# Gates by seven products of half-depth operands, with piecewise sums on VectorE and weight splits on GpSimd

## The chip, the cores and the metric

The kernel runs on one core of one Trainium2 chip. The metric is the device time of one launch in microseconds, the median of three runs: 2691.48 us for the kernel before (2688.23 to 2693.27). In the views, PE is TensorE (matmuls), PEld its weight loads, DVE is VectorE, ACT ScalarE, POOL GpSimd and SP SyncE, which issues most DMAs.

## What is computed

A decoder block on 2048 tokens of width 1024, in float32, cut here to what the change touches:

```
h = rmsnorm(x)
proj = h @ w_in                       # q, k, v, u, z, gate_a, gate_b
gate_a, gate_b = sigmoid(proj[GA0:GB0]), sigmoid(proj[GB0:IN_WIDTH])   # 1024 columns each
y_attn = dilated_attention(q, k, v)   # 3 groups of 4 heads, merged by a softmax over groups
y_gmlp = gelu(u) * spatial(layernorm(gelu(z)))
merged = gate_a * (y_attn @ w_branch_attn) + gate_b * (y_gmlp @ w_branch_gmlp)
x = x + rmsnorm(merged @ w_out)
x = x + rmsnorm(relu(rmsnorm(x) @ w_mlp_in)**2 @ w_mlp_out)
```

The change concerns the gates before their sigmoid: 2048 tokens by 1024 channels by 2048 columns.

## The kernel before

**Numbers in two parts.** TensorE takes operands that are rounded when written as `fp32r`. To keep float32's accuracy an operand is split in a high part (a rounded copy) and a low part (the rest): `split` (L66) writes the one on ACT or POOL (L70, L72) and the other on DVE or POOL (L78). A product of two operands is then three matmuls, high by high, high by low and low by high (L95 to L97). A group of three such matmuls, 128x128 weights on 512 columns, is called a step below. `h`, normalised and transposed, is kept split in SBUF as `hT`, one tile of 4 MB for each chunk `c` of 512 tokens; two such tiles fit. The tokens of chunks 0 and 1 are also kept in DRAM, unsplit (`hTd`), and come back by `reload_h` (L232), which splits them on POOL.

**The stages.** First (0 to some 500 us) the chunks are normalised and q, k and v are computed for each half of the tokens. Then comes the stage of gates and attention (some 500 to 1000 us), the merge of the attention groups (`combine`), the u and z of the first half, the gated merge, and the last two matrix products of the MLP, whose products are already formed by seven products.

**Filler.** Attention alone would leave TensorE waiting for exponentials. So the products of u, z and the gates are written as a generator, `filler` (L528), of which `steps(n)` takes the next n steps. The 16 gate blocks of 128 columns each, in two halves of the tokens, are 512 steps: for each block and chunk eight steps over the depth of 1024, summed in one PSUM bank, copied out by ACT (`gt`, L549) and stored in DRAM (`gated`, L551). Weights `w_g` come in blocks of 512 KB; POOL writes the high and DVE the low part.

**The attention units.** There are 48 units (three groups g, four chunks c, four heads j). A turn of the loop makes scores `s` of unit n, then one step, then the transposes `pT` of unit n-1, six steps (L781), its product with v (`pv`), two steps, and its last transposes `po`, which DVE sums (L709). Between, DVE adds the mask and takes the maxima (L653, L657), turns them into the bias `nm` (L660), ACT takes the exponentials (L663), copies `pT` (`ph`, L688, and `pf`, L696) and DVE makes its low part (L689). q and k of unit n+2 are loaded at each turn.

**Combine.** Behind the last unit `combine` (L714) loads the outputs `A` of all three groups for a chunk (L717, 528 KB each), works out the weights of the groups (`M`, `E`, `Z`, L720 to L733), sums them (L737 to L740) and TensorE transposes the mean (`yt`, L745). Steps (33, 21, 20, 24) stand ahead of the four chunks' transposes (L801).

**What sets the order.** TensorE runs in the order in which the program is written. The instructions of the other engines, SP's DMAs among them, are ordered by a scheduler from its own estimate of times, unless a stretch is bound by `behind()`, which keeps its instructions behind those already issued. Each engine then runs its list strictly in that order, SP too: a store that waits holds the loads behind it.

## Time and profile before

| | |
|---|---|
| median of 3 runs | 2691.48 us (2688.23 to 2693.27) |
| profiled execution | 2690.6 us |
| its span (first to last instruction) | 2688.7 us |
| granted TensorE clock over the span | 0.998 of full speed |
| DMA | 431.77 MB, 161 GB/s over the span |
| gates' copies on ACT (L549) | 64, 37.8 us |
| gates' low parts on DVE (L78) | 30, 45.1 us |
| gates' high parts on POOL (L72) | 32, 34.1 us |

The span is one execution taken by the profiler. Matmuls are pipelined: the duration given for one (390 ns for 128x512) overlaps its neighbours, so the time that one costs is the distance between two starts. A busy engine is not by itself a bound; what counts is whether TensorE, busy 99% of the span, has to wait. "DMA share" is the mean busy share of the core's 16 DMA engines.

### The profile page before, as it was taken

To read this page: it belongs to the slowest core of one execution; us is meant where nothing else is said; L and a number is where in the kernel's file an instruction comes from. 1 tells how busy PE (TensorE), PEld (TensorE's weight loads), DVE (VectorE), ACT (ScalarE), POOL (GpSimd) and SP (SyncE) were. 2 spreads that over 40 slices of the span, in tenths; PEclk is the share of its full clock that TensorE was granted. 3 is DMA by queue.
4 is the path that set the end of the run, shared out by engine and by line. 5 is a ranking of instruction groups with operands and counts; after the bars stand their busy time and mean duration, and the time that the engine had idled before them with its cause. 6 is when DMAs were issued, how large, how long until landed. Compare 5 with 4: busy or idle time off the path is not lost. (4 is left out here: it accounts for less than half of the span.)

```text
span 2688.7 us, 34842 instructions
## 1 busy us (share of the span) xinstructions
PE 2660.5 (99%) x12674; PEld 2225.8 (83%) x12674; DVE 1586.6 (59%) x2677; ACT 1052.1 (39%) x2149; POOL 975.7 (36%) x837
## 2 busy tenths in 40 slices
...
GB/s 272 167 143 183 153 141 211 103 189 201 173 252 203 219 152 195 185 181 147 180 250 250 141 205 163 186 171 129 110 145 118 87 55 87 93 84 86 90 110 211
DMA packets 299197, 431.77 MB, mean 161 GB/s; under 512 B 52817, under 2 KB 166225, under 8 KB 299026
## 3 DMA queue, kind: packets, MB, share of 16 engines
q1 hardware_dynamic: 226864, 370.48, 43.4%
q10 hardware_dynamic: 64178, 32.06, 4.0%
...
## 5 line engine op out<-in xcount | busy, mean ns | idle before, releaser
L1637 PE MATMUL ya<-T_spots,s 128*128 128x512 f32 x1176 | 289.3, 390 | 1.0 <-ACT T_spots L70 0.5
L1637 PEld LDWEIGHTS ya<-T_spots,s 128*128 128x128 f32 x1176 | 220.7, 188 | 47.4 <-ACT T_spots L70 0.9
L70 ACT ACTIVATE s<-sraw 128x768 fp32r<-128x768 f32 (+1 forms) x184 | 127.2, 696 | 330.3 <-POOL sraw L1438 155.8
L78 DVE TENSOR_TENSOR s<-sraw,s 128x512 fp32r<-128x512 f32 x172 | 184.2, 1095 | 8.5 <-ACT s L70 7.2
L1112 PE MATMUL aa<-B,A 128*128 128x512 f32 x768 | 182.1, 390 | 0.9 <-ACT xs L1126 0.9
L1112 PEld LDWEIGHTS aa<-B,A 128*128 128x128 f32 x768 | 144.0, 188 | 31.0 <-ACT xs L1126 1.3
L1637 PE MATMUL yc<-T_spots,s 128*128 128x512 f32 x624 | 159.7, 389 | 0.0
L72 POOL TENSOR_SCALAR w_g<-w_g_r 128x1024 fp32r<-128x1024 f32 x32 | 34.1, 1082 | 344.7 <-PE g L97 286.7
L1083 POOL TENSOR_TENSOR s<-w1r 128x512 f32<-128x512 f32 x32 | 42.9, 1342 | 311.9 <-DVE S L78 261.6
L95 PE MATMUL x<-hT_a,wq 128*128 128x512 f32 x384 | 149.8, 390 | 0.0
L96 PE MATMUL x<-hT_a,wq 128*128 128x512 f32 x384 | 149.6, 390 | 0.0
L97 PE MATMUL x<-hT_a,wq 128*128 128x512 f32 x384 | 149.6, 390 | 0.0
L709 DVE TENSOR_REDUCE o<-po 128x256 f32<-128x512 f32 x48 | 33.1, 691 | 184.9 <-PE po L708 184.9
L1637 PEld LDWEIGHTS yc<-T_spots,s 128*128 128x128 f32 x624 | 117.2, 188 | 24.3
L70 ACT ACTIVATE hl<-r 128x512 fp32r<-128x512 f32 x48 | 30.4, 632 | 238.1 <-POOL r L307 89.1
L78 POOL TENSOR_TENSOR T_spots<-w2r,T_spots 128x512 fp32r<-128x512 f32 x70 | 104.5, 1520 | 7.3 <-ACT T_spots L70 7.3
L95 PE MATMUL g<-hT_b,w_g 128*128 128x512 f32 x256 | 104.7, 409 | 0.0
L95 PE MATMUL o<-wo,mg 128*128 128x512 f32 x256 | 101.3, 396 | 3.4 <-DVE g L899 2.4
L95 PE MATMUL g<-hT_a,w_g 128*128 128x512 f32 x256 | 104.3, 407 | 0.0
L78 DVE TENSOR_TENSOR A<-w1r,A 128x512 fp32r<-128x512 f32 x61 | 62.6, 1026 | 68.6 <-ACT A L70 68.6
L70 ACT ACTIVATE S<-w1r 128x512 fp32r<-128x512 f32 x96 | 60.1, 629 | 106.3 <-PE ac L1112 63.9
L97 PE MATMUL o<-wo,mg 128*128 128x512 f32 x256 | 100.6, 393 | 0.0
(390 smaller groups left out, 7195.5 us busy)
## 6 DMA issues: line engine op xcount, KB each, us to landing
w1r<-in_w_mlp_in_dram SPq DMA_DIRECT2D x64, 512.0 KB, 3.7
sraw<-sd SPq DMA_DIRECT2D x128, 256.0 KB, 3.3
...
qq<-qk SPq DMA_DIRECT2D x96, 256.0 KB, 4.9
w_g_r<-in_w_in_dram SPq DMA_DIRECT2D x32, 512.0 KB, 4.8
gated<-gt SPq DMA_DIRECT2D x64, 256.0 KB, 3.3
...
sd<-u ACTq DMA_DIRECT2D x63, 256.0 KB, 3.8
```

The source lines that it names most:

```text
L70: act.activation(hi, src, AF.Copy)
L72: pool.tensor_scalar(hi, src, 1.0, 1.0, op0=OP.mult, op1=OP.mult)
L78: (pool if lo_eng == "pool" else dve).tensor_sub(lo, src, f32(hi))
L95: pe.matmul(ps, lh, rh, start=start, stop=False)
L96: pe.matmul(ps, lh, rl, start=False, stop=False)
L97: pe.matmul(ps, ll, rh, start=False, stop=stop)
L709: dve.tensor_reduce(ot[:, :, j * 64:(j + 1) * 64], po.rearrange("p (b h e) -> p b e h", b=4, h=2), axis=AX.X, op=OP.add)
L1083: pool.tensor_add(s1, a21, a22)
L1112: pe.matmul(p, w[:, l, k, :], h[:, r, k, :], start=i in (1, 6, 5) and not k and not n, stop=k == 3 and n == 2, skip_group_check=True)
L1637: pe.matmul(p, s[:, l], w[r], start=i in (1, 2, 5) and not m and not o, stop=m == 1 and o == 2, skip_group_check=True)
```

## The change

The gates are computed half by half of the tokens as a product of matrices of two by two blocks, with seven block products in place of eight. The blocks halve the depth (channels 0 to 511 and 512 to 1023), the columns (the two 128-column parts `m` of each of eight 256-column weight blocks `n`) and the tokens (two chunks). Each product has four steps, so there are 2 x 7 x 8 products and 448 steps.

- **Phases.** The products are taken in phases (1, 2), (6, 7), (5, 3), (4), each for all eight `n`, so that one phase needs one or two token operands. While one phase runs, `operand` loads those of the next into the other of two 4 MB places (`opA`, `opB`): split token blocks for products 1 to 3 from `hbd` (2 MB each), and sums of token blocks for the others from `tgd` (1 MB each). The latter are split on arrival by ACT (L70, 128x1024) and POOL (L78), two of each for an operand.
- **Pieces.** Each product's weights are a piece of 128x512 (256 KB, rows of 512 bytes), loaded four products ahead and split three products ahead, both parts on POOL.
- **Evacuation.** Products 1 and 2 are copied by ACT (32 copies); the five others are added by DVE to what an earlier product left (80 additions of 128x512). 1 and 2, 6 and 7, 5 and 3 lie in pairs, and products 1, 6, 5 and 4 start a PSUM bank, in which 2, 7 and 3 go on.
- **Sums ahead.** In the first part `pre_step` makes the sums of weight blocks (`sgd`, `s1gd`) and of token blocks (`tgd`): 32 turns, each with a load, four operations of 128x(256 or 2x128) on DVE and stores on POOL's queue. They are handed out one at each v block of the second half, two at each q or k product, and two at the end.
- **Tokens kept.** `keep_cols` now keeps all four chunks unsplit (16 more copies on ACT and stores), `prenorm_cols` also stores split tokens (`hbd`), and `reload_h` loads them split: 4 MB for a chunk in place of 2, and nothing to split.
- **Steps.** A turn of the attention loop takes 8 steps from the fourth unit on (5 in place of 6 between `pT` and `pv`), and `combine` takes (28, 18, 17, 19). u of the first half runs chunk by chunk.

The core of the diff:

```diff
...
-    hT_d = dtile([2, P, KT, 512], "hTd")
+    hT_d = dtile([4, P, KT, 512], "hTd")
+    hb_d = dtile([4, P, 2, KT, 512], "hbd")
+    tg_d = dtile([2, P, 4, 4, 512], "tgd")
+    sg_d = dtile([8, P, 2, 4, 256], "sgd")
+    s1g_d = dtile([8, P, 4, P], "s1gd")
...
+        if i == 3:
+            ks = slice(4 if c == 3 else 0, KT)
+            if c != 2:
+                for o in range(2):
+                    sp.dma_start(hb_d[c][:, o, ks], f32(h)[:, o, ks])
...
-            split_in(hT[c][:, :, k:k + 2], hT_d[c, :, k:k + 2, :], None, "pool", "pool")
+            for o in range(2):
+                sp.dma_start(f32(hT[c])[:, o, k:k + 2], hb_d[c][:, o, k:k + 2])
...
+        def pre_t(half, k, j):
+            w = pre.tile([P, 5, 256], F32, name=f"pt{half}{k}{j}", tag="pre")
+            tsl = slice(j * 256, (j + 1) * 256)
+            for c in range(2):
+                sp.dma_start(w[:, 2 * c:2 * c + 2], hT_d[2 * half + c][:, k::4, tsl])
+            yield
+            b11, b21, b12, b22 = (w[:, n] for n in range(4))
+            dve.tensor_sub(b11, b12, b11)
+            dve.tensor_sub(b12, b22, b12)
+            dve.tensor_sub(b22, b22, b11)
+            dve.tensor_sub(b21, b21, b22)
+            yield
+            pool.dma_start(tg_d[half][:, :, k, tsl], w[:, :4])
+            yield
+        def pre_s(n, k):
+            w = pre.tile([P, 5, 256], F32, name=f"ps{n}{k}", tag="pre")
+            both = w[:, :4].rearrange("p (h k) c -> p h (k c)", h=2)
+            sp.dma_start(both, a["w_in"][13 + n].rearrange("p (h k) c -> p h k c", h=2)[:, :, k:k + 2].rearrange("p h k c -> p h (k c)"))
+            yield
+            a11, a21, a12, a22 = (w[:, 2 * kk:2 * kk + 2, m * P:(m + 1) * P] for kk in range(2) for m in range(2))
+            s1 = w[:, 4].rearrange("p (k c) -> p k c", k=2)
+            dve.tensor_add(s1, a21, a22)
+            dve.tensor_sub(a21, a11, a21)
+            dve.tensor_sub(a11, s1, a11)
+            dve.tensor_sub(a12, a12, a11)
+            yield
+            pool.dma_start(sg_d[n][:, :, k:k + 2].rearrange("p h k c -> p h (k c)"), both)
+            pool.dma_start(s1g_d[n][:, k:k + 2], s1)
+            yield
+        halves = [[(h_, k, j) for k in range(4) for j in range(2)] for h_ in range(2)]
+        makers = [lambda n=n, k=k: pre_s(n, k) for n in range(8) for k in (0, 2)]
+        makers[12:12] = [lambda z=z: pre_t(*z) for z in halves[0] + halves[1]]
+        flow = []
+        def pre_step():
+            with behind():
+                if makers:
+                    flow.append(makers.pop(0)())
+                for g in reversed(flow):
+                    next(g)
+                if len(flow) == 3 or not makers:
+                    flow.pop(0)
...
+                if half:
+                    pre_step()
...
                 qk_pair(rp, w, g, which, 2 * half, ropes[2 * half])
+                pre_step()
...
                 qk_pair(rp, w, g, which, 2 * half + 1, ropes[2 * half + 1], between)
+                pre_step()
+        pre_step()
+        pre_step()
...
-    queue += [(13 + n, "g", n, 1) for n in range(8)] + [(13 + n, "g", n, 0) for n in range(8)]
+    queue += [(13, "g", 0, 1)]
     queue += [(9, "u", 0, 0), (10, "u", 1, 0), (11, "z", 0, 0), (12, "z", 1, 0)]
...
+    PHASES = ((1, 2), (6, 7), (5, 3), (4,))
...
+    PIECES, SPLITS, LAST = 4, 3, 104
+    seq = [(half, i, n) for half in (1, 0) for ops in PHASES for i, n in lagged(ops)]
+    g_ = dict(raw={}, w={}, b={})
+    def piece(t):
+        if t >= len(seq):
+            return
+        half, i, n = seq[t]
+        raws = g_["raws"]
+        r = raws[t % 4] if t < 8 else raws[4 + (t - LAST) % 5] if t >= LAST else raws[(t - 4) % 6]
+        if i < 3:
+            src = w_src(13 + n, i - 1)[:, :, :P]
+        elif i == 5:
+            src = s1g_d[n]
+        else:
+            kk, m = {6: (0, 0), 7: (0, 1), 3: (1, 0), 4: (1, 1)}[i]
+            src = sg_d[n][:, kk, :, m * P:(m + 1) * P]
+        sp.dma_start(r.rearrange("p (k c) -> p k c", k=4), src)
+        g_["raw"][t] = r
+    def split_piece(t):
+        if t >= len(seq):
+            return
+        if t == 4:
+            g_["spots"].append(wp.tile([P, 4, 2, 4, P], F32R, name="spots1", tag="w", bufs=3))
+        at_ = t % 4 if t >= LAST else t % 8
+        w = g_["spots"][at_ // 4][:, at_ % 4]
+        split(w[:, 0], w[:, 1], g_["raw"].pop(t).rearrange("p (k c) -> p k c", k=4), "pool", "pool")
+        g_["w"][t] = w
+    def operand(half, i, slot):
+        c = 2 * half
+        g_["b"][half, i] = slot
+        if i in (1, 2, 3):
+            src = hb_d[c + (i == 3)][:, :, (0, 4, 4)[i - 1]:][:, :, :4]
+            for o in range(2):
+                sp.dma_start(f32(slot)[:, o], src[:, o])
+            return []
+        src = tg_d[half][:, (5, 4, 7, 6).index(i)]
+        for k in range(0, 4, 2):
+            sp.dma_start(f32(slot)[:, 1, k:k + 2], src[:, k:k + 2])
+        return [(slot, k) for k in (0, 2)]
+    def gates_ahead():
...
+        for t in range(PIECES):
+            piece(t)
+        for t in range(SPLITS):
+            split_piece(t)
+    def gates():
+        bank, todo = {}, []
+        slots = [None, hp.tile([P, 2, 2, 4, 512], F32R, name="opB", tag="hT", bufs=2)]
...
+        g_["b"].update({(1, 1): hT[2][:, :, :4], (1, 2): hT[2][:, :, 4:]})
+        phases = [(half, ops) for half in (1, 0) for ops in PHASES]
+        starts, t = {}, 0
+        for n, (half, ops) in enumerate(phases):
+            starts[t] = n
+            t += 8 * len(ops)
+        for t, (half, i, n) in enumerate(seq):
+            if t in starts:
+                ph, t0 = starts[t], t
+                if ph + 1 < len(phases):
+                    s = (ph + 1) % 2
+                    if not slots[s]:
+                        slots[s] = hp.tile([P, 2, 2, 4, 512], F32R, name="opA", tag="hT", bufs=2)
+                    for j, i2 in enumerate(phases[ph + 1][1]):
+                        todo += operand(phases[ph + 1][0], i2, slots[s][:, j])
+                else:
+                    reload_h(0)
+                    want(5)
+            elif todo and (t - t0) % 3 == 1 and t > t0 + 1:
+                w, k = todo.pop(0)
+                with behind():
+                    split(w[:, 0, k:k + 2], w[:, 1, k:k + 2], f32(w)[:, 1, k:k + 2], "act", "pool")
+            piece(t + PIECES)
+            split_piece(t + SPLITS)
+            if i in (1, 6, 5, 4):
+                bank[n] = psum_mm(f"g{half}{i}{n}")
+            p, w, h = bank[n], g_["w"].pop(t), g_["b"][half, i]
+            for k in range(4):
+                for m, (l, r) in enumerate(((0, 0), (0, 1), (1, 0))):
+                    pe.matmul(p, w[:, l, k], h[:, r, k], start=i in (1, 6, 5, 4) and not k and not m,
+                              stop=k == 3 and m == 2, skip_group_check=True)
+                if t == 2 and late:
+                    sz_out(*late.pop(0))
+                yield
...
+            x, z = xs[n], zs[:, n]
+            if i == 1:
+                act.activation(x, p, AF.Copy)
+            elif i == 2:
+                act.activation(z, p, AF.Copy)
+                o = z, 0, 0
+            elif i == 6:
+                dve.tensor_add(z, x, p)
+            elif i == 7:
+                dve.tensor_add(x, x, p)
+            elif i == 5:
+                v = vs[n % 3]
+                dve.tensor_add(v, x, p)
+                o = v, 1, 1
+            elif i == 3:
+                dve.tensor_add(z, z, p)
+                o = z, 0, 1
+            else:
+                dve.tensor_add(x, x, p)
+                o = x, 1, 0
+            if i in (2, 5, 3, 4):
+                c = 2 * half + o[2]
+                sp.dma_start(gate_d[n * 2 + o[1], :, c * 512:(c + 1) * 512], o[0])
     def filler():
...
+            if kind == "g":
+                yield from gates()
+                continue
...
+                if not half and (ci, n) == (0, 0):
+                    reload_h(1)
...
-            steps(6 if n > 1 else 9)
+            steps((6 if n < 4 else 5) if n > 1 else 9)
...
-        steps((33, 21, 20, 24)[n])
+        steps((28, 18, 17, 19)[n])
...
```

At three places the lists of the engines show what moved. The first is an attention unit on ACT early in the stage, in the phase of products 1 and 2, from the copy of one `pv` to the next. Names: `ph` and `pf` are the copies of `pT`, `e` the exponentials, `gt` (before) and `ga`, `gz` (now) the gates' evacuation. Before:

```order
L704 ACTIVATE pvs_4450<-pv_4442 128x512
L688 ACTIVATE ph_4498<-pT_4493 128x512
L663 ACTIVATE e_4464,o_3746<-e_4464,nm_4479 128x128
L663 ACTIVATE e_4464,o_3746<-e_4464,nm_4479 128x256 x3
L688 ACTIVATE ph_4505<-pT_4501 128x256
L549 ACTIVATE gt_4516<-g_4432 128x512
L696 ACTIVATE pf_4508<-pT_4501 128x128
L704 ACTIVATE pvs_4549<-pv_4541 128x512
```

Now:

```order
L904 ACTIVATE pvs_4731<-pv_4723 128x512
L700 ACTIVATE gz<-g_4618 128x512
L70 ACTIVATE opB<-opB 128x1024
L888 ACTIVATE ph_4787<-pT_4782 128x512
L863 ACTIVATE e_4745,o_4055<-e_4745,nm_4760 128x128
L863 ACTIVATE e_4745,o_4055<-e_4745,nm_4760 128x256 x3
L888 ACTIVATE ph_4794<-pT_4790 128x256
```

The gates' copy of the one unit stands ahead of `ph` now, not ahead of `pf`, and an operand's split stands with it.

The second is SP's list behind the last unit's output (`att_76`), where combine's loads of `A` stand. Before:

```order
L583 DMA att_76<-o_8002 128x1056 [waits DMAHW6_49,DVE_49]
L551 DMA gated<-gt_8701 128x512 [waits DMAHW7_49,Activation_49]
L717 DMA A_8614<-att_74 128x4x264 [waits DMAHW6_49,DMAHW0_49,PE_49]
L717 DMA A_8614<-att_75 128x4x264 [waits DMAHW1_49]
L717 DMA A_8614<-att_76 128x4x264 [waits DMAHW2_49]
```

Now:

```order
L718 DMA gated<-gx_4365 128x512 [waits DMAHW1_49,DVE_49]
L783 DMA att_76<-o_8402 128x1056 [waits DMAHW2_49,DVE_49,Activation_49]
L718 DMA gated<-ga_4489 128x512 [waits DMAHW3_49,DVE_49]
L718 DMA gated<-ga_4490 128x512 [waits DMAHW4_49,DVE_49]
L91 DMA w_u_r_9190<-in_w_in_dram 128x1024 [waits DMAHW5_49,Pool_49]
L917 DMA A_9047<-att_74 128x4x264 [waits DMAHW6_49,DMAHW2_49]
L917 DMA A_9047<-att_75 128x4x264 [waits DMAHW7_49]
L917 DMA A_9047<-att_76 128x4x264 [waits DMAHW0_49]
```

One gate store stood between the output and the loads; now there are two and a load of `w_u`, and ahead of them the reload of a chunk's tokens.

The third is DVE's list there, from the last sum of `po` (L709, now L909) to combine's first operation on `A` (`M`, L720, now L920). Before:

```order
L709 TENSOR_REDUCE o_8002<-po_8551 128x4x64
L709 TENSOR_REDUCE o_8002<-po_8602 128x4x64
L78 TENSOR_TENSOR w_u_8877<-w_u_r_8878,w_u_8877 128x1024
L78 TENSOR_TENSOR w_u_8877<-w_u_r_8882,w_u_8877 128x1024
L720 TENSOR_TENSOR M_8618<-A_8614 128x16
```

Now:

```order
L909 TENSOR_REDUCE o_8402<-po_9035 128x4x64
L714 TENSOR_TENSOR ga_4489<-ga_4489,g_9028 128x512
L714 TENSOR_TENSOR ga_4490<-ga_4490,g_9129 128x512
L714 TENSOR_TENSOR ga_4491<-ga_4491,g_9144 128x512
L714 TENSOR_TENSOR ga_4492<-ga_4492,g_9159 128x512
L78 TENSOR_TENSOR w_u_9189<-w_u_r_9190,w_u_9189 128x1024
L714 TENSOR_TENSOR ga_4493<-ga_4493,g_9174 128x512
L920 TENSOR_TENSOR M_9051<-A_9047 128x16
```

Five sums of gate products and a weight split stand ahead of `M`, where two weight splits did.

53 lines of the change are left out of this document (34 added, 19 removed).

## Prediction

> **What bounds the kernel now.** I read the page first, then who waits for whom on TensorE, then stretches of the span.
>
> ```profile
> PE 2660.5 (99%) x12674; PEld 2225.8 (83%) x12674; DVE 1586.6 (59%) x2677; ACT 1052.1 (39%) x2149; POOL 975.7 (36%) x837
> DVE 0%; issue 0%; ACT 0%; DVEq 0%
> ```
>
> TensorE is busy 99% of the span. The chain that ended last names only work at 0%, so it says nothing; what counts is the number of matmuls and the places where TensorE has nothing to do. In the gate and attention stage (560 to 1000 us) the view of waits has almost none:
>
> ```profile
> PE pT L683 <- DVE o L709: 1.3, 2, 0.6
> PE pv L702 <- DVE ph L689: 0.3, 1, 0.3
> ```
>
> That is 1.6 us in 440, and no better cover in this stage can win more than that. A matmul left out there is a gain of its own pitch, as long as the other engines and the DMAs still keep up. The pitch comes from a full stretch that has 128x512 matmuls alone; columns are busy us and counts for PE, PEld, DVE, ACT, POOL, then granted clock, DMA share, GB/s:
>
> ```profile
> 1650.00:1700.00 50.00, 50.00 (x222) 41.45 (x221) 22.28 (x30) 25.97 (x44) 11.00 (x8) 1.00 0.45 137
> 560.00:700.00 140.00, 139.04 (x818) 121.06 (x817) 58.56 (x178) 64.31 (x195) 8.28 (x8) 1.00 0.61 188
> 700.00:850.00 150.00, 149.37 (x864) 129.53 (x863) 68.37 (x202) 67.98 (x211) 42.33 (x28) 1.00 0.74 220
> 850.00:985.00 135.00, 134.89 (x749) 115.10 (x749) 47.69 (x189) 53.56 (x170) 8.25 (x8) 1.00 0.64 177
> 750.00:800.00 50.00, 50.00 (x291) 43.48 (x290) 21.43 (x67) 23.89 (x76) 34.07 (x20) 1.00 0.84 272
> ```
>
> 50 us / 222 = 0.225 us a matmul (the 390 ns that the page gives for one is its pipelined length).
>
> **What is removed.** Gates took 16 x 2 x 2 x 8 x 3 = 1536 matmuls; seven products of half the depth take 2 x 7 x 8 x 4 x 3 = 1344. 192 x 0.2252 us = **43.2 us** less, all in a stage where TensorE never rests. That is the gain if all else is covered. The profiled execution took 2690.6 us (its span 2688.7, 1.9 around it), 0.9 under the median, so the floor is 2690.6 - 43.2 = 2647.4 us.
>
> **Evacuation and splits.**
>
> ```profile
> L549 ACT ACTIVATE gt<-g 128x512 f32<-128x512 f32 x64 | 37.8, 592 | 62.8 <-PE g L97 42.6 <-issue 10.0 <-DMA ygd<-sb 4.8
> L78 DVE TENSOR_TENSOR w_g<-w_g_r,w_g 128x1024 fp32r<-128x1024 f32 x30 | 45.1, 1522 | 46.3 <-POOL w_g L72 46.3
> L1642 DVE TENSOR_TENSOR acc_yt<-acc_yt,ya 128x512 f32<-128x512 f32 x72 | 48.4, 684 | 24.2 <-PE ya L1637 24.2
> L72 POOL TENSOR_SCALAR yt<-yt x6: 614/618/880, 1083.6 to 1092.3; 128x512 fp32r<-128x512 f32 x6
> L78 POOL TENSOR_TENSOR yt<-yt x6: 1272/1292/1341, 1084.6 to 1094.1; 128x512 fp32r<-128x512 f32 x6
> ```
>
> DVE loses 45.1 us of splits and gains 80 additions from PSUM, 80 x 0.684 = 54.7 us: even. ACT loses 64 and gains 32 copies, about -19 us, and gains 16 operand splits of 128x1024 (an estimate from the 0.592 us of half that width: 1.05 us). POOL gains most: 112 pieces x (0.618 + 1.292) = 214 us and 16 operand splits of 2.4. Spread over the stage (some 385 us) POOL is busy about 65%; the stretch 750:800 has it at 34 us of 50 and TensorE at 50.00, so its mere load costs nothing.
>
> What POOL can do is hold DVE. In the three rows of `nm` below, the same 128x4 operation takes 0.17 us with POOL idle, and 0.86 and 1.94 us with POOL at work; it ends when POOL's instruction does:
>
> ```profile
> 703.70 0.17 DVE L660 TENSOR_SCALAR nm<-o 128x4 f32<-128x4 f32 x1
> 769.00 0.86 DVE L660 TENSOR_SCALAR nm<-o 128x4 f32<-128x4 f32 x1
> 778.28 1.94 DVE L660 TENSOR_SCALAR nm<-o 128x4 f32<-128x4 f32 x1
> 777.81 4.75 POOL L78 TENSOR_TENSOR w_g<-w_g_r,w_g 128x1024 fp32r<-128x1024 f32 x2
> 708.05 0.88 PE L702 MATMUL pv<-ph,v 128*128 128x256 f32 x6
> 707.38 0.27 ACT L696 ACTIVATE pf<-pT 128x128 f32<-128x128 f32 x1
> ```
>
> Behind `nm` on ACT stand the exponentials and `pf`, and `pv` waits for `pf`. In this unit `pf` is ready at 707.65, and its first use is the end of the `pv` row's six matmuls, at 708.76: 1.1 us to spare, of which the gate copy ahead of `pf` on ACT takes 0.5. The change takes a step of three matmuls (0.68 us) from between `pT` and `pv`, and in most phases the copy too. So about 0.9 us is left against a hold of at most 1.3 us (a piece) or 2.4 us (an operand split). The bounds: nothing, since the delayed units of 769 to 788 us show no wait; or 0.4 us in each of 32 units and 1.5 us at each of 16 operand splits, 37 us. Only a part of the units meets a POOL instruction at its start, and the last 16 units use `pf` another way, with more room. I take **4 us**, nearer the lower row.
>
> The Trainium skill (GPSIMD Engine Reference, Key points) says that GpSimd shares its SBUF interfaces with VectorE and contends with DVE instructions in a 2-port mode or with two SBUF inputs. The rows of `nm` agree for the first kind. By the rule as it stands the piecewise sums, with two SBUF inputs each, would be slowed as well; at one and a half times their length this adds some 22 us to DVE in a part where it idles far more, and changes the sum by nothing.
>
> **DMA.** In the three stretches above the DMAs are busy 85 + 111 + 86 = 283 us of 425 and move 83 MB.
>
> ```profile
> q1 hardware_dynamic: 226864, 370.48, 43.4%
> q10 hardware_dynamic: 64178, 32.06, 4.0%
> ```
>
> Packets of 500 bytes (q10) take 0.040 x 2688.7 x 16 / 64178 = 27 ns, 3.3 us per MB on 16 engines; q1 as a whole 3.15 us per MB. The gates' pieces are 112 x 0.262 = 29.4 MB in packets of 512 bytes, 96 us, in place of 16.8 MB, 53 us; the operands add 16.8 MB, 53 us. So 283 + 96 = 379 us of busy time in about 385: a share of 0.98, by 112 MB / 385 us = 290 GB/s. That is the dearest doubt. For it speaks that 750:800 ran 272 GB/s at 0.84 with TensorE at 50.00, and that a stretch below (1150 to 1160) moved 374 GB/s. Against it, every queue of loads gets longer and an operand of up to 4 MB comes in one burst. A piece is asked for four products ahead, some 17 us among the units, against 4.8 us to landing and 1.9 us of POOL:
>
> ```profile
> sraw<-sd SPq DMA_DIRECT2D x128, 256.0 KB, 3.3
> w_g_r<-in_w_in_dram SPq DMA_DIRECT2D x32, 512.0 KB, 4.8
> hT_b<-hTd SPq DMA_DIRECT2D x8, 512.0 KB, 6.9
> ```
>
> Bounds: nothing; or, if no more than 0.93 can be had, 379 / 0.93 - 385 = 22 us. I take **5 us**, since the stage before ran at 0.84 free of loss.
>
> **Sums in the first part.**
>
> ```profile
> 300.00:500.00 200.00, 200.00 (x882) 165.31 (x881) 92.73 (x113) 27.69 (x42) 70.84 (x43) 1.00 0.46 152
> ```
>
> 128 operations of 256 columns at about 0.34 us (the row of L737 below: 4.11 / 12) are 44 us of DVE in 450, with DVE at about half and DMA at half: covered. Weight splits on DVE can slip by two or three of these; where there is little room, 0 to 3 us; I take **1**. The start of the gates depends on POOL, which splits three pieces in 5.7 us right behind the last u and z work: 0 to 2, I take **1**.
>
> **The combine behind the last unit** is the one stall that I can follow row by row:
>
> ```profile
> 985.46 0.60 PE L708 MATMUL po<-ident,pvs 128*128 128x128 f32 x4
> 990.61 5.07 SPq L717 DMA_DIRECT2D A<-att  x6
> 996.99 0.17 DVE L720 TENSOR_TENSOR M<-A 128x16 f32<-128x16 f32 x1 [3.10 <-DMA A<-att]
> 1000.62 4.11 DVE L737 TENSOR_TENSOR A<-A,E 128x256 f32<-128x256 f32 x12
> 1005.90 1.23 DVE L740 TENSOR_TENSOR A<-A 128x1024 f32<-128x1024 f32 x1
> L745 PE MATMUL yt<-ident,A x32: 270/273/273, 1008.4 to 1056.1; 128*128 128x128 f32 x32
> ```
>
> From `po` to the loads of `A` 5.15 us, to `M` 11.5, to the end of the mean 21.7; TensorE asks for it at 22.9, after 33 steps. In the changed kernel only 28 steps lie there: 28 x 0.676 + 0.6 = 19.5 us. On SP the loads of `A` stand behind the store of the second product after `po` (2 x 2.7 + 0.7 = 6.1 us) and a load of `w_u`; on DVE `M` stands behind the sum of the fifth product (5 x 2.7 + 0.7 = 14.2 us) and the split of that `w_u`. So the mean ends between 21.7 (as before) and 14.2 + 10.1 = 24.3, and TensorE waits 2 to 5 us. I take 4 for this and the next `yt`. What then comes on top is the clock:
>
> ```profile
> 1110.00:1120.00 10.00, 7.75 (x49) 6.88 (x48) 8.55 (x13) 6.41 (x10) 1.72 (x2) 0.96 0.93 313
> 1120.00:1130.00 10.00, 10.00 (x44) 8.42 (x43) 7.76 (x11) 2.54 (x3) 2.95 (x2) 0.87 0.69 218
> 1140.00:1150.00 10.00, 7.63 (x34) 6.03 (x33) 6.46 (x9) 5.76 (x9) 0.00 (x0) 1.00 0.82 294
> 1150.00:1160.00 10.00, 10.00 (x39) 8.07 (x38) 8.12 (x13) 7.24 (x12) 0.00 (x0) 0.83 1.00 374
> ```
>
> 2.3 us without work were followed by 10 us at 0.87 and at 0.83, 1.3 to 1.7 us lost. I add 1: **5 us** in all, bounds 0 and 9. The Trainium skill (TensorE: Matmul & The Clock Gate, What's actually happening) lets the clock fall only after an idle window of about 3.4 us; by it a stall of 2 to 3 us would be free of this and the sum 1 us lower. The two rows show a fall after less, and the measurement decides.
>
> **The sum:** 2690.6 - 43.2 + 4 + 5 + 1 + 1 + 5 = **2663 us**, own range 2653 to 2674.
>
> **Rivals.**
>
> *All is covered* (15%): 2647 to 2653. For it: 750 to 800 us. Against: the 28 steps of the combine.
>
> *The DMAs set the pace of the late units* (20%): 2674 to 2685. The 22 us above in place of 5 give 2680. For it: a share of 0.98. Against: units have loads in hand, and the stretch at 374 GB/s.
>
> *About no change* (7%): 2685 to 2696. POOL holds `nm` in every unit (37 us in place of 4, hence 2696, or somewhat less).
>
> *Slower* (16%): packets of 512 bytes are dearer as loads beside the attention's own than q10's as stores. The room is 385 + 43 - 283 = 145 us for the extra traffic, of which operands less old weights take none; 145 us x 16 / 57344 packets = 40 ns. From 40 ns a packet on the stage lasts longer than before. At 45 ns the pieces take 161 us, the stage 444 in place of 385: 2663 - 5 + 59 = 2717. Against it: the stretch 1650:1700, fed mostly by loads of 256 KB, takes 0.45 x 50 / 6.85 MB = 3.3 us per MB, as q10 does.
>
> My forecast has 42%. A difference under 0.2% (5.4 us) can't be told from none. Faster has 15 + 42 + 20 = 77%, no change 7%, slower 16%. The range reaches from the floor to where the gain ends, 2647 to 2690, and leaves out the slower case and a little on either side.
>
> **What would show it.** Right: 192 fewer 128x512 matmuls in the gates' rows; TensorE waits of a few us for `pT` or `pv`, scattered, with `nm` at over 1 us; one wait of 2 to 5 us for `A` ahead of `yt` at about 960 us; DMA share above 0.9 in the units. Wrong: waits of `g` for pieces (`spots`) or operands, many small ones adding up to over 15 us, which would mean DMA or POOL is late; or no wait ahead of `yt`. A wait in the first part for split weights would show the piecewise sums in the way.

## The result, and the profile after

Nothing was won: the changed kernel takes 2691.05 us (median of 12 runs, 2686.51 to 2698.77) beside 2690.43 us for the kernel before (12 runs, 2688.23 to 2697.29). The ratio is 1.0003, 95% interval 0.9993 to 1.0013. The profiled execution took 2693.69 us, its span 2692.0.

From the page of the kernel after, its first section:

```profile
PE 2629.0 (98%) x12482; PEld 2196.3 (82%) x12482; DVE 1657.3 (62%) x2855; ACT 1061.1 (39%) x2151; POOL 1189.2 (44%) x1075
```

TensorE has exactly 192 matmuls fewer (12674 - 12482), and it is busy 31.5 us less. The time stayed, so it waits or runs slower. Two views tell where. First, stretches of the kernel after (columns as in the prediction: busy us and counts for PE, PEld, DVE, ACT, POOL, then clock, DMA share, GB/s):

```profile
570.00:925.00 355.00, 354.98 (x2091) 308.60 (x2090) 175.04 (x571) 166.60 (x514) 192.46 (x183) 1.00 0.89 264
950.00:1000.00 50.00, 42.58 (x194) 33.95 (x193) 15.72 (x33) 6.61 (x22) 16.15 (x15) 0.93 0.74 251
1000.00:1050.00 50.00, 30.17 (x129) 24.30 (x127) 29.25 (x86) 13.59 (x18) 14.62 (x7) 0.83 0.95 313
```

Then who TensorE waits for, up to 1130 us (total, times, longest; `issue` means that the profile names nobody: the first `yt` starts at 1010.44, as DVE ends the mean of `A` at 1010.34):

```profile
PE yt L945 <- POOL A L940: 11.4, 2, 10.8
PE yt L945 <- issue: 8.8, 1, 8.8
PE g L686 <- POOL spots L72: 5.7, 2, 3.3
PE pt L218 <- ACT hr L237: 4.4, 1, 4.4
PE s L836 <- DMA kp<-qk: 3.4, 1, 3.4
PE sz L545 <- DVE z L573: 3.2, 3, 2.1
```

Among the attention units from 570 to 925 us TensorE is busy 354.98 of 355 us; nothing is lost there. Every wait of this list stands at an end: in the first part (`pt`, copies of the tokens), at the start of the gates (`sz`), and from 927 us on (`kp`, `spots`, then `yt` of the combine).

A table made from the trace puts sizes to this. Its marks are the starts of TensorE's instructions: the first `sz` group (behind it the gates start), the first transposes `po` of a unit, those of the 43rd and of the last unit, the four chunks' `yt`, and the third `sz` group, ahead of the gated merge. "Due" is before less 0.2252 us for each matmul that the stage has lost.

| stage, us | before | matmuls lost | due | after | after less due |
|---|---|---|---|---|---|
| to the first `sz` | 504.6 | 0 | 504.6 | 512.0 | +7.4 |
| to the first `po` | 51.7 | 0 | 51.7 | 57.4 | +5.7 |
| 42 units | 387.4 | 120 | 360.4 | 357.4 | -3.0 |
| last five units | 41.7 | 15 | 38.3 | 53.4 | +15.1 |
| last `po` to first `yt` | 22.9 | 15 | 19.5 | 30.2 | +10.7 |
| to the second | 15.2 | 9 | 13.2 | 16.4 | +3.2 |
| to the third | 14.5 | 9 | 12.5 | 23.5 | +11.0 |
| to the fourth | 17.2 | 15 | 13.8 | 15.3 | +1.5 |
| to the third `sz` | 51.4 | 9 | 49.4 | 49.4 | 0 |
| sum up to this mark | 1106.7 | 192 | 1063.5 | 1115.1 | +51.6 |

Behind the mark both kernels run the same instructions: 1581.9 us before, 1576.9 after. In the kernels below this rest lay between 1576 and 1585 us, one profiled execution each, so single executions are compared up to the mark and times by their medians. Kernels below whose edits lie behind it reach the first `sz` at 509.5 to 513.1 us, so 2 or 3 us in one stage of one execution say nothing. (Rows and sum are rounded one by one.)

Of the 51.6 us, 37.8 are TensorE idle (43.8 us up to the mark, 6.0 before, from the gaps between its records); the other 13.8 are mostly a lower clock behind the stops. An estimate of it, the busy time of each 10 us times what the granted clock lacks there, gives about 12 us up to the mark, and 0.3 us before. The granted clock is 0.71 from 1010 to 1020 us and 0.83 from 1050 to 1060. The rows show it: after 8.8 us without work the next matmuls stand 0.43 us apart, not 0.225, until 1015.94 us; after 10.85 us until 1053.41. The matmuls behind both, from TensorE's timeline of the kernel after (start, duration, operation; in brackets idle before and releaser):

```profile
1012.61 0.63 PE L96 MATMUL u<-hT_b,w_u 128*128 128x512 f32 x1
1013.03 0.63 PE L97 MATMUL u<-hT_b,w_u 128*128 128x512 f32 x1
...
1015.94 0.39 PE L95 MATMUL u<-hT_b,w_u 128*128 128x512 f32 x1
...
1050.38 1.97 PE L945 MATMUL yt<-ident,A 128*128 128x128 f32 x8 [10.85 <-POOL A L940]
...
1053.41 0.39 PE L95 MATMUL u<-hT_b,w_u 128*128 128x512 f32 x1
```

The Trainium skill (TensorE: Matmul & The Clock Gate, What's actually happening) has the clock at half after an idle window of about 3.4 us and back after as long a time of work. The pitch of 0.43 us agrees with the half. Counted from the end of the stop it lasts 5.5 us (1010.44 to 1015.94) and 3.0 us (1050.38 to 1053.41), so the time of the return is only near the page's.

### What holds the combine

SP's list of the kernel after, from its timeline (start, time of the issue; `x8` means eight DMAs in a row):

```profile
975.03 5.06 SPq L245 DMA_DIRECT2D hT_b<-hbd  x7
...
985.97 0.32 SPq L783 DMA_DIRECT2D att<-o  x1
...
993.22 5.59 SPq L917 DMA_DIRECT2D A<-att  x6
...
1003.18 2.84 SPq L245 DMA_DIRECT2D hT_b<-hbd  x2
...
1013.00 2.89 SPq L91 DMA_DIRECT2D w_z_r<-in_w_in_dram  x2
1015.95 1.37 SPq L245 DMA_DIRECT2D hT_b<-hbd  x3
...
1026.12 3.72 SPq L917 DMA_DIRECT2D A<-att  x3
```

The first loads of `A` are issued 13.0 us behind the last `po` (980.2) in place of 5.15. They go out as the store of the last output (`att<-o`) lands. Two parts of that chain grew: DVE ends its last sum of `po` 5.7 us behind it (985.9) in place of 1.3, and the store takes 7.2 us to land in place of 3.1. DVE's sum in the kernel before, then the store's row of the DMA view (KB, us to landing), before and after:

```profile
986.10 0.69 DVE L709 TENSOR_REDUCE o<-po 128x256 f32<-128x512 f32 x1 [7.26 <-PE po L708]
```

```profile
att<-o SPq DMA_DIRECT2D x1, 528.0 KB, 3.1
```

```profile
att<-o SPq DMA_DIRECT2D x1, 528.0 KB, 7.2
```

The first reload, issued from 974 us on, is still landing until 989.2; that it slows the store is likely (in e14, where the store goes 9 us behind the reload's last issue in place of 6, it lands in 3.2 us), but no run shows it apart.

The third chunk's loads wait until 1026.12, 15.7 us behind the first `yt`, which frees their buffer. In the kernel before it was 1.1 us (1008.4; SP's list before):

```profile
1009.47 0.38 SPq L717 DMA_DIRECT2D A<-att  x1
```

In the kernel after, the second reload and the loads of `w_u` and `w_z` (L91) stand ahead of them, and those of L91 are the ones that wait long, four times and 14.0 us in all; the two longest, from SP's waits from 1000 to 1030 us:

```profile
SPq L91 <- DVE w_z L78: 4.7, 1, 4.7
SPq L91 <- DMA w_u_r<-in_w_in_dram: 4.6, 1, 4.6
```

POOL and DVE show the rest (two timelines of the kernel after):

```profile
967.04 0.62 POOL L72 TENSOR_SCALAR spots<-ga 128x512 fp32r<-128x512 f32 x1 [23.21 <-DMA ga<-sgd]
976.30 0.62 POOL L72 TENSOR_SCALAR spots<-ga 128x512 fp32r<-128x512 f32 x1 [7.29 <-DMA ga<-sgd]
...
1045.54 2.34 POOL L939 TENSOR_TENSOR A<-A 128x1024 f32<-128x1024 f32 x1 [18.74 <-DMA ud<-ut]
```

```profile
979.32 3.59 DVE L78 TENSOR_TENSOR w_u<-w_u_r,w_u 128x1024 fp32r<-128x1024 f32 x2 [20.43 <-POOL w_u L72]
...
985.23 0.68 DVE L909 TENSOR_REDUCE o<-po 128x256 f32<-128x512 f32 x1
...
1000.20 0.18 DVE L920 TENSOR_TENSOR M<-A 128x16 f32<-128x16 f32 x1 [1.60 <-DMA A<-att]
...
1037.93 0.17 DVE L920 TENSOR_TENSOR M<-A 128x16 f32<-128x16 f32 x1 [15.84 <-DMA A<-att]
```

In the last units POOL stands 23.21 and 7.29 us for a piece (`ga<-sgd`). The split of `w_u` stands behind these pieces on POOL, its other half holds DVE (20.43 us), and the last output `o` is done only at 985.9. The piece itself waits on SP for its place, as SP's waits from 940 to 1060 us say:

```profile
SPq L613 <- DMA gated<-ga: 14.4, 3, 6.0
```

`piece` gives products from 104 on five places, three of them the tiles `vs`. These hold the sums of product 5, whose stores (`gated<-ga`) are not over when the piece is due.

### The profile page after: what moved, and what is told of

It is laid out like the page before. It is cut to its first block, busy times and chain, and to the rows that moved or that the text cites. A ratio compares the mean times of both kernels' runs of the same rounds, so it can differ in the third digit from the quotient of the medians.

```text
span 2692.0 us, 35404 instructions
## 1 busy us (share of the span) xinstructions
PE 2629.0 (98%) x12482; PEld 2196.3 (82%) x12482; DVE 1657.3 (62%) x2855; ACT 1061.1 (39%) x2151; POOL 1189.2 (44%) x1075
## 3 DMA queue, kind: packets, MB, share of 16 engines
q1 hardware_dynamic: 302224, 435.51, 50.4%
## 5 line engine op out<-in xcount | busy, mean ns | idle before, releaser
L70 ACT ACTIVATE s<-sraw 128x768 fp32r<-128x768 f32 (+1 forms) x184 | 127.2, 696 | 330.5 <-POOL sraw L1641 155.5
L78 DVE TENSOR_TENSOR s<-sraw,s 128x512 fp32r<-128x512 f32 x172 | 184.1, 1095 | 8.5 <-ACT s L70 8.5
L686 PE MATMUL g<-opB,spots 128*128 128x512 f32 x576 | 150.7, 404 | 7.4 <-POOL spots L72 5.7
L686 PE MATMUL g<-opA,spots 128*128 128x512 f32 x576 | 149.0, 400 | 0.0
L686 PEld LDWEIGHTS g<-opB,spots 128*128 128x128 f32 x576 | 104.8, 192 | 28.2 <-POOL spots L72 6.3
L70 ACT ACTIVATE hl<-r 128x512 fp32r<-128x512 f32 x48 | 30.4, 633 | 234.9 <-POOL r L316 89.0
L686 PEld LDWEIGHTS g<-opA,spots 128*128 128x128 f32 x576 | 103.5, 189 | 18.0
L1640 POOL TENSOR_TENSOR sraw<-sraw 128x256 f32<-128x256 f32 x56 | 41.8, 747 | 162.0 <-DVE s L78 159.0
L78 POOL TENSOR_TENSOR T_spots<-w2r,T_spots 128x512 fp32r<-128x512 f32 x70 | 104.4, 1520 | 7.3 <-ACT T_spots L70 7.3
L909 DVE TENSOR_REDUCE o<-po 128x256 f32<-128x512 f32 x48 | 33.2, 691 | 112.9 <-PE po L908 112.9
L70 ACT ACTIVATE S<-w1r 128x512 fp32r<-128x512 f32 x96 | 60.1, 629 | 106.9 <-PE ac L1315 63.8
L72 POOL TENSOR_SCALAR spots<-gr 128x512 fp32r<-128x512 f32 x72 | 44.8, 623 | 129.0 <-PE g L686 72.0
## 6 DMA issues: line engine op xcount, KB each, us to landing
w1r<-in_w_mlp_in_dram SPq DMA_DIRECT2D x64, 512.0 KB, 3.8
wq_r<-in_w_in_dram SPq DMA_DIRECT2D x24, 512.0 KB, 4.7
```

The source lines that it names most:

```text
L70: act.activation(hi, src, AF.Copy)
L72: pool.tensor_scalar(hi, src, 1.0, 1.0, op0=OP.mult, op1=OP.mult)
L78: (pool if lo_eng == "pool" else dve).tensor_sub(lo, src, f32(hi))
L686: pe.matmul(p, w[:, l, k], h[:, r, k], start=i in (1, 6, 5, 4) and not k and not m, stop=k == 3 and m == 2, skip_group_check=True)
L909: dve.tensor_reduce(ot[:, :, j * 64:(j + 1) * 64], po.rearrange("p (b h e) -> p b e h", b=4, h=2), axis=AX.X, op=OP.add)
L1640: pool.tensor_add(a22, a21, a22)
```

## The experiments

All 18 kernels are the changed one with small edits. Times are medians; the ratios are to the kernel before, run on the same chip beside them, with 95% intervals. Stages are those of the table above.

**e1: other places for the last pieces.** The three tiles are used in the order in which their stores end.

```diff
-                g_["raws"] += a[8:] + vs
+                g_["raws"] += a[8:] + [vs[2], vs[0], vs[1]]
```

> Only the order changes in which the pieces of the last phase take the three places that hold product 5's sums: the place whose store is oldest first. Theory (the last phase's pieces wait for stores of sums, each load three products too late): TensorE's waits for spots between 960 and 985 us, 6.7 us with the steps between them, are gone; the last unit takes about 8 us from po to po in place of 17.3; total 8 to 11 us less than the changed kernel, about 2681. Rival (the DMAs are full there, so pieces are late whatever the place): the last unit stays above 14 us, total within 3 us of 2691.

2691.14 us, 1.0000 [0.9991, 1.0009]. The last five units fell from 53.4 to 44.1 us, so the places made most of their stall (38.3 were due). But `yt` then came 34.7 us behind the last `po` in place of 30.2: half of the stall moved on. DVE ended its last sum 5.7 us behind the last `po` as in after, but the output's store was issued 3.2 us later still (979.24), behind the reload and stores of gate sums in SP's list, and took 9.1 us to land. The split of a `w_u` block ahead of `M` on DVE, which the list shown with the change has too, held almost nothing: it ended at 994.3, and `M` started at 994.83, while the second of the loads that it needs landed only at 994.7.

**e2: the reload unsplit**, 2 MB a chunk, split by ACT and POOL on arrival.

```diff
-            for o in range(2):
-                sp.dma_start(f32(hT[c])[:, o, k:k + 2], hb_d[c][:, o, k:k + 2])
+            split_in(hT[c][:, :, k:k + 2], hT_d[c, :, k:k + 2, :], None, "act", "pool")
```

> reload_h brings the unsplit tokens (2 MB a chunk) as in the kernel before, split by ACT and POOL, in place of 4 MB of split ones. Theory (8 MB of reload in the stretch of combine hold the store of the last output and the loads of A): the first yt comes 22 to 26 us after the last po in place of 30.2, the third 15 to 19 us after the second in place of 23.5; total 8 to 18 us less, about 2678. Rival (the place of the loads of A in SP's list decides, not the bytes): both distances as they are, total within 4 us of 2691.

2696.53 us, 1.0024 [1.0014, 1.0033]. The third `yt` comes 14.2 us behind the second (23.5 in after), but the splits stand in ACT's list and wait for their loads, with the attention's copy behind them:

```profile
PE po L907 <- ACT pvs L903: 17.1, 1, 17.1
```

**e3: the loads of A issued by ACT**, past SP's list.

```diff
-            sp.dma_start(A[:, :, g, :], att_d[g][c * 512:(c + 1) * 512, :].rearrange("(n p) e -> p n e", p=P))
+            act.dma_start(A[:, :, g, :], att_d[g][c * 512:(c + 1) * 512, :].rearrange("(n p) e -> p n e", p=P))
```

> The loads of A are issued by ACT in place of SP, nothing else. Theory of bytes (reload fills the DMAs): the first yt still comes about 30 us after the last po, since the store of the last output lands late; the third moves by less than 5 us; total 0 to 5 us less. Rival (SP's list holds them: the third chunk's loads are issued 14 us after their buffer is free): the third yt comes 13 to 17 us after the second in place of 23.5; total 8 to 14 us less, about 2680.

2687.60 us, 0.9984 [0.9972, 0.9996]. The third `yt` needs 17.0 us in place of 23.5 with all bytes left in place: it was the place in the list. The first `yt` stays at 1010.0 us, and of the 8 to 14 us that the rival expected in total, 3.5 came.

**e4: the `sz` group six steps (one and a half products) later**, to give z's normalisation time.

```diff
-                if t == 2 and late:
+                if (t, k) == (3, 2) and late:
```

> The products sz of the last z chunk are put 6 steps later among the gates' first steps. Theory (POOL's first splits hold DVE's normalisation of z, 4.05 us for four rows in place of 1.92, and TensorE waits for it): the wait of sz for z, 3.2 us in all, is gone, and with it the clock of 0.83 behind it; from the first sz to the first po 52 to 53 us in place of 57.5; total 4 to 6 us less, about 2686. Rival (the pieces are late as well, so the wait moves): a wait for spots or opB of 2 us or more in its place, total within 2 us of 2691.

2702.00 us, 1.0044 [1.0029, 1.0059]. The wait for z is gone, and a dearer one stands in its place (`sz` to `po` 66.6 us); in e4:

```profile
PE g L686 <- POOL spots L72: 15.3, 3, 12.1
```

**e5: four turns of the sums in the first part moved to its end.**

```diff
-                pre_step()
+                if half or n < 4:
+                    pre_step()
...
-        pre_step()
-        pre_step()
+        for _ in range(6):
+            pre_step()
```

> The four turns of the piecewise sums that fall on the last two q and k products of the first half (about 185 to 225 us) are made at the end of the first part instead. Theory (their loads and stores stand in SP's list and on full DMAs ahead of the stores of the kept columns hr, whose three buffers then run out, so the transposes pt wait): the wait of pt for hr, 4.4 us, and the clock of 0.71 behind it are gone; the first sz comes 5 to 7 us earlier, at 504 to 507 us; total 4 to 7 us less, about 2685. Rival (the copies kept of chunk 2 and their 256 KB stores are by themselves too much for the three buffers): pt still waits 3 us or more, total within 3 us of 2691.

2694.48 us, 1.0015 [1.0005, 1.0025]. `pt` no longer waits for `hr` (4.4 us in after): the turns of the sums did hold it. By the rows it was in part through SP's list, where a load of theirs takes 4.09 us to issue ahead of the stores of `hr`. The DMAs are full there as well (a share of 1.02 and 1.08 from 205 to 225 us), and e5 doesn't tell the two apart. SP's rows of the kernel after, then ACT's:

```profile
215.57 4.09 SPq L445 DMA_DIRECT2D ps<-in_w_in_dram  x1
219.76 1.84 SPq L238 DMA_DIRECT2D hTd<-hr  x3
```

```profile
225.05 1.09 ACT L237 ACTIVATE hr<-pt 128x512 f32<-128x512 f32 x2 [4.70 <-DMA hTd<-hr]
```

In e5 a wait of the same length came at the end, where the six turns now stand:

```profile
PE rowsum L533 <- POOL wsp L528: 4.4, 1, 4.4
```

**e6: the first three pieces split by ACT and DVE.**

```diff
-            split_piece(t)
+            split_piece(t, "act", "dve")
```

> The first three pieces are split by ACT and DVE in place of POOL, nothing else. Theory (POOL's splits hold DVE's normalisation of z: 4.05 us for the four L573 in place of 1.92, and its small operations up to 1.3 us in place of 0.17): the four take 2 to 2.6 us, the wait of sz for z falls from 3.2 to under 1.2 us; first sz to first po 53 to 55 us in place of 57.5; total 2 to 5 us less. Rival (sz simply asks too early, 8 steps sooner behind z than before): the wait stays over 2.5 us whatever POOL does, total within 2 us.

2695.21 us, 1.0016 [1.0006, 1.0025]. The four operations on z still take 4.05 us: a miss, POOL's splits at that time are those of the next four pieces.

**e7 and e8: e1 and the reload unsplit, split by POOL; e8 with the loads of A on ACT too.**

```diff
+            split_in(hT[c][:, :, k:k + 2], hT_d[c, :, k:k + 2, :], None, "pool", "pool")
...
+            act.dma_start(A[:, :, g, :], att_d[g][c * 512:(c + 1) * 512, :].rearrange("(n p) e -> p n e", p=P))
```

> The order of places of e1_last_pieces, and the reload of unsplit tokens (2 MB a chunk), split by POOL alone so that ACT is not held by a load. Theory (bytes of reload, and lists held by loads): the last unit takes 8 to 11 us, the first yt comes 22 to 28 us after the last po, the third 14 to 17 us after the second; total 12 to 22 us less than the changed kernel, about 2674. Rival (pieces behind the reload on POOL become the wait): waits for spots of 6 us or more behind the last units, total within 6 us of 2691.

> e7_reload_pool with the loads of A issued by ACT. Theory of bytes: e7 has the gain, this one differs from it by less than 4 us. Rival (the place in SP's list decides): 6 us or more less than e7, the first yt 22 to 25 us after the last po.

2701.17 us, 1.0039 [1.0024, 1.0054], and 2702.51, 1.0042 [1.0028, 1.0057]. The last pieces now stand behind the reload's splits on POOL (e7):

```profile
PE g L685 <- POOL spots L72: 8.9, 2, 6.7
...
PE g L685 <- POOL spots L78: 6.4, 5, 3.3
```

**e9: no reload at all.** u and z of the first half read a gate operand that lies in SBUF; the reloaded tokens are left out of the computation.

```diff
+    class Kept:
+        def __init__(self, slot):
+            self.slot = slot
+        def __getitem__(self, at_):
+            return self.slot[:, 0, at_[1], at_[2] % 4, at_[3]]
...
-                    reload_h(0)
+                    hT[0] = hT[1] = Kept(slots[0])
...
-                if not half and (ci, n) == (0, 0):
-                    reload_h(1)
```

> The two reloads of split tokens (8 MB) are left out; u and z of the first half are computed from an operand that still lies in SBUF, so these parts of the output are not the reference's. Nothing else changes. Theory (the reload in the stretch of combine takes the DMAs and SP's list from the loads of A): the first yt comes 23 to 27 us after the last po in place of 30.2, the third 13 to 16 us after the second in place of 23.5, and the total is 12 to 20 us less than the changed kernel, about 2676. Rival (SP's order and the waits for pieces make the loss without the bytes): first and third yt within 4 us of their places, total within 6 us of 2691.

2692.27 us, 1.0002 [0.9993, 1.0012]. It gains 11.0 us at the third `yt` (12.5) and loses 12.3 between the fourth and the third `sz` (61.7 us), where POOL, then TensorE, waits for the merge's operand:

```profile
1100.09 0.91 POOL L72 TENSOR_SCALAR yt<-yt 128x512 fp32r<-128x512 f32 x1 [29.19 <-DMA yt<-yad]
```

So the stall at the third `yt` goes when the reload goes. But the edit takes away the bytes and the places in SP's list at once, and it couldn't show their worth. Probably the merge's loads wait for the operand's space, which the edit keeps in use to the end of z; that was not tried apart. The first `yt` came at 1010.2 us as in after, and this doesn't clear the first reload: the output's store landed in 5.0 us in place of 7.2, but two more splits of `w_u` had moved ahead of DVE's last sum of `po`, which came 11.7 us behind the last `po` in place of 5.7.

**e10: e1, and the reload unsplit with its splits behind the last unit**, `w_u`'s second block, `w_z` and the second reload kept behind loads of A.

```diff
-            for o in range(2):
-                sp.dma_start(f32(hT[c])[:, o, k:k + 2], hb_d[c][:, o, k:k + 2])
+            sp.dma_start(f32(hT[c])[:, 1, k:k + 2], hT_d[c, :, k:k + 2])
+    def resplit_h(c):
+        for k in range(0, KT, 2):
+            split(hT[c][:, 0, k:k + 2], hT[c][:, 1, k:k + 2], f32(hT[c])[:, 1, k:k + 2], "act", "dve")
...
+            if (kind, n, half) == ("u", 0, 0):
+                with behind():
+                    want(q + 1)
...
-            if (kind, n) == ("u", 1) or (kind, n, half) == ("u", 0, 0):
+            if (kind, n) == ("u", 1):
...
+                    with behind():
+                        reload_h(1)
+                if not half and (ci, n) == (0, 1):
+                    with behind():
+                        resplit_h(1)
+                if not half and (ci, n) == (1, 0):
+                    with behind():
+                        want(q + 2)
...
+    with behind():
+        resplit_h(0)
```

> The tokens are reloaded unsplit (2 MB a chunk) and split by ACT and DVE behind the last unit, when they have landed; the loads of w_u (second block), w_z and the second reload stand behind the loads of A in SP's list; the last pieces' places as in e1_last_pieces. Theory (three things together make the loss behind the units: pieces waiting for stores, 8 MB, and loads ahead of A in the list): last five units 42 to 46 us in place of 53.4, first yt 20 to 25 us after the last po, third yt 13 to 16 us after the second; total 18 to 28 us less than the changed kernel, 2663 to 2673. Rival (the waits only move, as in e7_reload_pool: u waits for the split tokens): the sum from the last po to the fourth yt stays at 82 us or more, total 2682 or more.

2679.37 us, 0.9962 [0.9949, 0.9975]: faster than both kernels. The last five units take 41.6 us, the first `yt` comes at 1000.2 us, the third after 20.0. The time lies above the range of the theory and below the rival's.

**e11 and e12: the front.** e11 moves four turns of the sums to the first q and k products of the second half and has ACT and DVE split pieces 3 to 6; e12 is e10 and e11 together.

```diff
+                if half or n < 4:
+                    pre_step()
...
+                if half and n < 4:
+                    pre_step()
...
+            split_piece(t + SPLITS, *(("act", "dve") if t < 4 else ()))
```

> Four turns of the piecewise sums are moved from the end of the first half to the first q and k products of the second half, and pieces 3 to 6, whose splits fall on the normalisation of z, are split by ACT and DVE in place of POOL. Theory: pt no longer waits for hr, the first sz comes at 504 to 507 us in place of 512; the four L573 take 1.9 to 2.4 us in place of 4.05 and sz waits under 1 us; first sz to first po 52 to 54 us in place of 57.4; total 8 to 13 us less, about 2680, if the waits behind the units do not take it back. Rival (other waits take their place, as in e5_sums_later): first po within 4 us of 569 us.

> e10_split_late and e11_front together. Theory: the gains add, since they lie in separate stretches: 28 to 40 us less than the changed kernel, 2651 to 2663, clear of the kernel before. Rival (TensorE's gain is taken back behind the units wherever it is made): 2675 or more.

2699.08 us, 1.0026 [1.0015, 1.0036], and 2685.91, 0.9983 [0.9974, 0.9992]. The four operations on z, in after and then in e11:

```profile
527.83 4.05 DVE L573 TENSOR_SCALAR z<-z,mv,r_ln 128x512 f32<-128x512 f32 x4
```

```profile
527.10 1.92 DVE L577 TENSOR_SCALAR z<-z,mv,r_ln 128x512 f32<-128x512 f32 x4
```

POOL's splits beside them were the cause of the doubled time. Yet neither start got shorter (513.0 and 60.8 us), since e11 waits elsewhere:

```profile
PE g L690 <- POOL spots L72: 9.7, 3, 4.1
PE x L95 <- DVE t L312: 5.7, 2, 4.4
```

**e13: e1 and the order alone.** As e10, but the reload as the change has it: 8 MB, split, nothing to do on arrival.

```diff
+            if (kind, n, half) == ("u", 0, 0):
+                with behind():
+                    want(q + 1)
...
+                    with behind():
+                        reload_h(1)
+                if not half and (ci, n) == (1, 0):
+                    with behind():
+                        want(q + 2)
```

> The places of the last pieces as in e1 and the order of SP's list as in e10 (w_u's second block, w_z and the second reload behind the loads of A); the reload is left as the change has it, 8 MB of split tokens from hbd, with no splits. Theory 'order': what stands ahead of the loads of A in SP's list made the stalls, not the bytes; then last five units 41 to 43 us, first transposes of the combine 30 to 32 us behind the last unit, third 18 to 21 us, and the time 2678 to 2683 us as in e10. Theory 'bytes' (8 MB and the order both count; leaving out the bytes alone gained nothing because the order was left): third 22 us or more, the time 2686 to 2691 us.

2681.04 us, 0.9957 [0.9940, 0.9974]. It differs from e1 (1.0000) in nothing but the order of loads, with the splits of `w_u` and `w_z` that follow them, and from e10 in the bytes and splits. Its profiled execution is the slowest of its four (2687.33 us). The third `yt` takes 16.6 us in place of 24.6, since its loads are issued earlier; SP's list in e13:

```profile
997.02 0.92 SPq L91 DMA_DIRECT2D w_u_r<-in_w_in_dram  x2
998.65 9.08 SPq L245 DMA_DIRECT2D hT_b<-hbd  x8
...
1012.42 3.70 SPq L924 DMA_DIRECT2D A<-att  x3
```

In e1 these loads of `A` were issued at 1021.34 us. The whole second reload, 4 MB, stands ahead of them here too; only the loads of `w_z` stand behind them now, and nothing of L91 stops the list. The first `yt` (1005.9 us) is no earlier than e1's (1005.1); in e10 it comes at 1000.2. There the first reload is four DMAs ahead of the last output's store, not eight. The store in e10, then in e13:

```profile
975.41 0.32 SPq L797 DMA_DIRECT2D att<-o  x1
```

```profile
980.83 0.32 SPq L790 DMA_DIRECT2D att<-o  x1
```

Of these 5.4 us the last `po` accounts for 2.2 (969.2 and 971.4 us). DVE's last sum ends 6.2 us behind it in both (975.4 and 977.6); e10 stores it at once, e13 3.3 us later, behind the longer reload in SP's list. So the first reload costs something too, by its issues or by its bytes, and e10 gives the gain back at the third `yt` (20.0 us), where DVE splits the second.

**e14: e10 with the old places.**

```diff
-                g_["raws"] += a[8:] + [vs[2], vs[0], vs[1]]
+                g_["raws"] += a[8:] + vs
```

> e10 with the last pieces' places as the change has them (three tiles that hold sums of product 5 still being stored). If the places make the stall of the last five units, these take 50 us or more instead of 41.6, but the first transposes of the combine come at about the same time as in after or some us earlier, so that the time is 2683 to 2688 us. Rival: with half the bytes of the reload in the way the stores end in time; then the last five take under 45 us and the time is that of e10, 2679 us.

2685.51 us, 0.9980 [0.9971, 0.9990]. The last five take 49.4 us. By the medians the places are worth 6 us once the combine doesn't take them back, though the two intervals just overlap.

**e15: e10 with the sums of the combine on DVE alone.**

```diff
-        eng = dve if c in (1, 2) else pool
+        eng = dve
```

> e10 with the combine's sums of all four chunks on DVE (two were on POOL, 3.65 + 2.41 and 6.92 + 2.44 us there, the third at the time in which TensorE waits). Theory 'POOL beside DVE': DVE takes about 2 us for the same pair, so the third's transposes come 3 to 6 us earlier (20.0 to 15 us) and the time is 2674 to 2677 us. Rival (hT_b's splits on DVE make that stall, DVE is the one that is late): DVE's further work makes it no shorter, 2679 to 2683 us.

2684.43 us, 0.9978 [0.9966, 0.9989]. Not better: the third `yt` took 22.7 us, `u` waited 8.3 us for `hT_b`'s splits on DVE (5.9 in e10). The rival held, with a time 1.4 us above its range.

**e16: e10 with more steps ahead of the first `yt`.**

```diff
-        steps((28, 18, 17, 19)[n])
+        steps((40, 14, 14, 14)[n])
```

> e10 with 40, 14, 14 and 14 steps ahead of the combine's four groups of transposes in place of 28, 18, 17 and 19. Theory 'too few steps': the first group waits 7.0 us for its data while steps stand behind it, and twelve steps are about 8.5 us; then the idle time ahead of it goes, the two middle groups have their data as long as they have it now, and the time is 2671 to 2675 us. Rival: the steps moved ahead need the reloaded tokens and the second block of w_u, which come behind the loads of A, so that TensorE waits for these instead (u<-hT_b or w_u ahead of the first group); the time is 2677 to 2684 us.

2686.05 us, 0.9984 [0.9975, 0.9993]. The steps moved ahead need the rest of `w_u`, as the rival said, with a time 2 us above its range:

```profile
PE u L95 <- POOL w_u L72: 5.6, 1, 5.6
```

**e17 and e18: the first reload as in e10, the second as in e13; e18 stores the last output from ACT's queue.**

```diff
+            for o in range(2) if c else (1,):
+                sp.dma_start(f32(hT[c])[:, o, k:k + 2], hb_d[c][:, o, k:k + 2] if c else hT_d[c, :, k:k + 2])
...
+        (act if (g, c) == (2, 3) else sp).dma_start(odst, ot_[g, c])
```

> e10 for the first reload (unsplit, split by ACT and DVE behind the last unit), e13 for the second (4 MB from hbd behind the first loads of A, nothing to split); w_u's second block and w_z as in both. If the order is the cause and the second reload's splits on DVE made the 5.9 us wait of u for hT_b in e10, that wait goes and the third group of transposes comes as in e13 (15 to 17 us in place of 20.0), the first as in e10 (30 to 32 us), and the time is 2674 to 2679 us. Rival: the larger second reload (4 MB ahead of the third chunk's loads of A) makes these late as in after; third 20 us or more, the time 2679 to 2684 us.

> e17 with the last unit's output stored from ACT's queue, not behind three gate stores in SP's list (975.4 us in e10, 2.5 us behind DVE's last sum of po). If that place in the list counts, the whole chain to the mean comes 1 to 2.5 us earlier, the first transposes 28.5 to 30.5 us behind the last unit, and the time is 1 to 3 us below e17. Rival: the loads of A then stand behind a store that waits for the next sum of gates on DVE, and nothing is won: within 1 us of e17.

2681.92 us, 0.9967 [0.9954, 0.9979], and 2680.67, 0.9962 [0.9949, 0.9976]. e17's third `yt` takes 16.6 us as in e13, e18's first comes 28.1 us behind the last `po` (30.8 in e17). Both stages came out as expected, but e18's not by the store's place in the list: in e17, too, the store goes 0.1 us behind DVE's last sum. e17's time lies above its forecast, and in total neither can be told from e10 or e13, whose intervals overlap theirs.

The stages of the main kernels side by side, with the sum up to the third `sz`:

| | to `sz` | to `po` | last five | 1st `yt` | 2nd | 3rd | 4th | to 3rd `sz` | sum | median |
|---|---|---|---|---|---|---|---|---|---|---|
| before | 504.6 | 51.7 | 41.7 | 22.9 | 15.2 | 14.5 | 17.2 | 51.4 | 1106.7 | 2690.4 |
| after | 512.0 | 57.4 | 53.4 | 30.2 | 16.4 | 23.5 | 15.3 | 49.4 | 1115.1 | 2691.1 |
| e1 places | 510.3 | 58.5 | 44.1 | 34.7 | 16.1 | 24.6 | 16.5 | 49.4 | 1111.7 | 2691.1 |
| e9 no reload | 510.7 | 58.8 | 48.3 | 35.2 | 14.7 | 12.5 | 13.8 | 61.7 | 1112.9 | 2692.3 |
| e10 | 511.4 | 58.9 | 41.6 | 31.0 | 15.3 | 20.0 | 13.8 | 50.4 | 1099.7 | 2679.4 |
| e13 order | 513.1 | 57.8 | 43.1 | 34.5 | 15.2 | 16.6 | 15.4 | 50.7 | 1103.8 | 2681.0 |
| e18 | 511.3 | 58.8 | 44.3 | 28.1 | 15.5 | 16.6 | 16.7 | 49.8 | 1098.4 | 2680.7 |

The 42 units between took 387.4 us before and 357.3 or 357.4 in all others.

## Why the prediction was wrong

**What is removed: right.** 192 matmuls are gone, and the units, which lost 120 of them, gained 30.0 us, 3.0 more than 120 x 0.2252.

**Attention units (4 us) and DMA (5 us): nothing was lost.** POOL does hold `nm`, in mean 344 ns (270 before), and the DMAs are busy 0.89 at 264 GB/s from 570 to 925 us, but TensorE has no wait there, up to the last five units. The rivals "the DMAs set the pace" and "POOL holds `nm` in every unit", both placed here, fell. So did 512-byte packets as a cause of a slower kernel.

**Sums in the first part (1 us) and the start of the gates (1 us): right places, wrong sizes**, +7.4 and +5.7. The prediction took room on DVE and POOL's three first splits as the price. By e6 it is not those three splits but the next four that fall on z. What stood in the way was a turn's load ahead of the tokens' stores (that the turns do it is shown by e5, where the wait vanishes) and POOL slowing a neighbour's work on DVE (shown by e11). The lower clock is in these numbers; two stretches behind the stops:

```profile
225.00:235.00 10.00, 9.30 (x36) 7.78 (x37) 6.09 (x11) 6.51 (x15) 4.13 (x4) 0.71 0.90 287
530.00:540.00 10.00, 9.01 (x47) 8.14 (x48) 4.79 (x7) 0.60 (x1) 5.41 (x5) 0.83 0.84 292
```

**The combine behind the last unit (5 us, bounds 0 and 9): the step that failed.** It stood at +15.1 in the last five units and +26.4 in the combine (10.7 + 3.2 + 11.0 + 1.5), 41.5 of the 51.6 us. Three things were left out of its sum:

- The last units were taken as undisturbed. The last pieces' places were in the diff, and the wait "of `g` for pieces" was named as what would show the prediction wrong, but no term priced it. e1 and e14 show it: 9.3 and 7.8 us of that stage.
- The chain to the first `yt` was counted from the last `po` with before's 5.15 us to the loads of `A`, and added a place or two behind them in SP's and DVE's lists. It took 13.0 us, and by the output's store, not by those places: DVE's last sum came 5.7 us behind the last `po` in place of 1.3, behind a split of `w_u` that POOL had delayed and sums of gates, and the store landed in 7.2 us in place of 3.1. `M`, which the prediction had wait for DVE's sums and a split, waits for `A` in after (1.60 us) and starts as it lands. This is read from the rows; no run sets DVE's last sum right (5.2 to 11.7 us behind the last `po` in all of them).
- Only the first `yt` was followed. For the next one nothing was worked out, and the dear one was the third: its loads of `A` stand behind the second reload and `w_z`, whose loads wait. e3 takes the loads of `A` out of that list, e9 the reload, e13 the loads of `w_z`, and the third falls from 23.5 to 17.0, 12.5 and 16.6 us.

The clock, put at 1 us, cost about 12 us up to the mark over all stops (the estimate above).

**The rival "about no change"** had the right time and the wrong mechanism: that it came out is luck.

**What stays open.** Order and places give back 10 to 12 us of the 51.6, and no kernel here mended the front. e5 and e11 moved its waits instead of removing them. The first `yt` still waits 6 to 7 us in e10 and e18. e11's and e6's times (2699.1, 2695.2) are 8 and 4 us over after's with no stage up to the mark to account for it; in their profiled executions the rest behind the mark is longer (1583.9 and 1582.4 us beside 1576.9), where nothing was changed, and the cause is not known.
